# A tail that normalises tiles as they lie in DRAM, and a new order of expert units

## The chip, the cores and the metric

The kernel runs on one core of a Trainium2 chip: TensorE (matmuls), VectorE, ScalarE, GpSimd, SyncE (which here only issues DMAs) and 16 DMA engines. Time is device microseconds of one execution, the median of several. In the trace the engines are PE (its weight loads PEld), DVE, ACT, POOL and SP.

## The reference, cut to what matters

One layer of a diffusion trunk on 1024 tokens of 1024 channels, all in float32: a mixer, then a mixture of 32 experts (top 1 of 4 groups, in it the top 2 of 8 experts), then the final norm. The part that the change touches:

```
gates = einsum('tk,tke->et', weights, one_hot(eid, 32))        # two experts per token
def body(acc, (wi, wo, ge)):
    a, u = split(t @ wi, 2)                                    # wi (1024, 512)
    return acc + ((silu(a) * u) @ wo) * ge[:, None]            # wo (256, 1024)
x = x + gt_m * sum over experts                                # residual
return rmsnorm(x, final_norm_g)                                # y * rsqrt(mean(y^2) + 1e-6) * g
```

A row of the output is final only when both experts of its token have been added to the residual stream.

## The kernel before, in words

The mixer writes the residual stream x2 to a DRAM tensor `x2_d` (1024 rows of 4 KB) and the normalised rows to `h2_d`. A routing stage then makes, for each expert, a list of its tokens' row numbers (`idx`) and weights (`wtab`). The expert stage, from about 520 us to the end, works on blocks of up to 128 rows. A block holds the tokens of one expert, or of two to three experts side by side in column groups. Its steps are methods of `Block`:

- `gather` (L1623): GpSimd fetches the block's rows from `h2_d` with an indirect DMA.
- `rows` (L1644 to L1650): TensorE transposes them, VectorE and ScalarE copy the result.
- `w1` (L1659), `gate`, `gate_T`: first product, SwiGLU, transpose.
- `products2` (L1683, L1688): second product; VectorE multiplies it by the weights into a tile `y`, of which there are two.
- `scatter` (L1701): GpSimd adds the rows of `y` into `x2_d` with one accumulating indirect DMA per expert in the block. All of these write the same tensor, so each waits on GpSimd until the one before has landed.

The weights, 6 slabs of 512 KB per expert, are streamed by SyncE through a ring of 42 slabs in SBUF (L1280), in the order of use.

The unit of order is a number `u`. Units 0 to 3 are two experts of 64 rows with one scatter; 4 to 7 are two experts (up to 96 and 32 rows) and 8 to 11 two experts (up to 64 and 64), with two scatters each; 12 to 18 are one expert. Unit 18 is followed by a merged block of three parts: the overflow of the two largest experts (rows beyond 128) and one small expert, so three scatters, of which only the small expert brings new weights. `ORDER` (L45) lists the units; the last of them, 11, is treated apart. The loop over units keeps TensorE's queue in the order w1 of the next unit, transposes of the one after, w2 of this unit; the other engines' queues are sorted by a scheduler. A generator `extra_blocks` plans the overflow (which rows the merged block takes, and whether further blocks are needed); the loop takes one step of it at three places per unit, and what is left is done at once before the merged block is gathered. A loop after the tail (L1896 on) does further blocks; with these inputs it runs no turn.

The tail (from L1816) does not scatter the last block. It loads the eight tiles of `x2_d` (L1836), builds eight selection matrices from the last block's row numbers (L1841), and adds the last block's rows to each tile by matmuls: four tiles wholly in PSUM (L1857, L1861; `PSUM_X2`), four by an add on VectorE (L1863). ScalarE squares (L1875), GpSimd takes the power -1/2 (L1880), VectorE multiplies by it and by the final gain `fgb` (L1884), SyncE writes the tile out (L1885).

Of the kernel before, what the change touches and what calls it, by code (L numbers as in the profile page):

```python
# [8 lines left out]
F32 = mybir.dt.float32  # L9
F32R = mybir.dt.float32r  # L10
BF = mybir.dt.bfloat16
I32 = mybir.dt.int32
U32 = mybir.dt.uint32
AF = mybir.ActivationFunctionType
# [27 lines left out]
          *range(NS + 9, NS + 13), *range(NS + 17, E), NS + 4]  # L42

FIXED = [*range(9, 16, 2), *range(25, 32, 2)]
ORDER = [0, 1, 2, 3, 13, 4, 14, 8, 15, 5, 17, 18, 9, 6, 12, 10, 7, 16, 11]  # L45
NDB = 2
N_W0 = 3
N_W1 = 2
N_W2 = 3
NXB = 3  # L50
BIG = 1.0e6
PSUM_X2 = (0, 3, 5, 7)

O_ID, O_MF, O_MB, O_CF, O_CB, O_DM, O_LE = (128 * j for j in range(7))
O_IND = 896
# [79 lines left out]
def hybrid_layer(ctx, tc, x, c, ctx_in, c_ctx, w_ada, b_ada, norm1_g, w_in, w_decay, b_decay, gla_norm_g,  # L135
# [1095 lines left out]
    def finish_idx(ix, tokens):  # L1231
        ve.tensor_scalar(ix, tokens, BIG, None, op0=OP.add)
# [233 lines left out]
    def order_tables():  # L1466

        pe = bank(0, 2, 1)
        te.matmul(pe[0:1, 0:E], lhsT=tok0[0:E], rhs=M, start=True, stop=True)
        ve.tensor_scalar(eid, pe[0:1, 0:E], -1.0, None, op0=OP.add)  # L1470
        pt = bank(7)
        for a in range(2):
            te.transpose(pt[0:E, a * P:(a + 1) * P], tfin[:, a], ident)
        tT = mo.tile([E, 2, P], F32, name="tT", bufs=1)
        ve.tensor_copy(tT, pt[0:E, 0:2 * P].rearrange("p (a n) -> p a n", a=2))
        pt = bank(0, 2, 1)
        te.matmul(pt[:, 0:ND], lhsT=tT[:, 0], rhs=M[:, NS:], start=True, stop=True)
# [9 lines left out]
        finish_idx(here, h)  # L1487
        finish_idx(idx[:, NS:], pt[:, 0:ND])
        ve.tensor_copy(wtab[:, 0:U_Y], w[:, 0:U_Y])
        ve.tensor_copy(wtab[96:P, U_Y:], w[96:P, U_Y:])  # L1490
# [283 lines left out]
    with tc.manual_schedule(engines={mybir.EngineType.PE}):  # L1774
        for _ in range(NXB):
            gather()
        expert_order()
        next(row_order).rows()
        for n in range(-1, len(units) - 2):
            u, v, w = (units[n + k] if 0 <= n + k < len(units) else [] for k in range(3))  # L1780
            for kk in range(2):
                for b in v:
                    b.w1(kk)
            for b in u:
                b.gate_T()
            if n < 0:
                order_tables()
                gather()
                for h in range(2):
                    pt = bank(0, 2, 1)  # L1790
                    spread(pt, gm8, 4 * h)
                    sc.activation(gtm[:, h * 512:(h + 1) * 512], pt, AF.Copy)
            for b in v:
                b.w1(2)
            if n >= 1:
                next(extra, None)
            todo = len(w)
# [10 lines left out]
            if n >= 1:  # L1808
                next(extra, None)
            for b in u:  # L1810
                b.w2()
            if n >= 1:
                next(extra, None)

    u, (last,) = units[-2:]
    with tc.manual_schedule(engines={mybir.EngineType.PE, mybir.EngineType.Pool, mybir.EngineType.DVE,  # L1816
                                     mybir.EngineType.Activation}):
        for b in u:
            for j in (4, 5):
                list(b.weights(j))  # L1820
        for j in range(6):
            list(last.weights(j))
        for b in u:
            b.gate_T()
            b.w2()
        kept += staging
        fgb = next_slab()
        for h in range(2):
            pt = bank(0, 2, 1)
            spread(pt, fg8, 4 * h)  # L1830
            sc.activation(fgb[:, h * 512:(h + 1) * 512], pt, AF.Copy)
        y1 = [next_slab() for i in range(NT)]
        jk = next_slab()
# [3 lines left out]
        m = last.m  # L1837
        sel = wst.tile([P, NT, P], F32R, name="hl", bufs=2)
        yp = [wst.tile([P, D], F32R, name="wraw", tag="wraw", bufs=2)[0:m] for k in range(2)]
        for i in range(NT):  # L1840
            ve.tensor_scalar(sel[:, i], iota, float(i * P), here, op0=OP.add, op1=OP.is_equal)  # L1841
        for j in range(4):
            last.w1(j)
        last.gate()
        last.gate_T()
        y = last.products2()
        for n in range(2):
            ns = slice(n * 512, (n + 1) * 512)
            split(yp[0][:, ns], yp[1][:, ns], y[:, ns])
        pts, ss = {}, {}  # L1850

        def add(i):

            pts[i] = [bank(5, 3, 7, 6, 4, 0, 2, 1) for n in range(2)]
            on_pe = i in PSUM_X2
            for n in range(2 * on_pe):
                te.matmul(pts[i][n], lhsT=ident, rhs=y1[i][:, n * 512:(n + 1) * 512], start=True, stop=False)  # L1857
            for n in range(2):
                ns = slice(n * 512, (n + 1) * 512)
                for k in range(2):  # L1860
                    te.matmul(pts[i][n], lhsT=sel[0:m, i], rhs=yp[k][:, ns], start=(k == 0 and not on_pe), stop=(k == 1))  # L1861
                if not on_pe:
                    ve.tensor_tensor(y1[i][:, ns], pts[i][n], y1[i][:, ns], OP.add)  # L1863

        def sums(i):

            if i in PSUM_X2:
                return [(pts[i][n], slice(n * 512, (n + 1) * 512)) for n in range(2)]
            return [(y1[i], slice(0, D))]

        def tile_stats(i):
            s = mo.tile([P, 2], F32, name="ss3", bufs=3)
            ss[i] = s[:, 0:1]
            for n, (t, ns) in enumerate(sums(i)):
                sc.activation(jk[:, ns], t, AF.Square, scale=D ** -0.5, accum_out=s[:, n:n + 1])  # L1875
            if i in PSUM_X2:
                ve.scalar_tensor_tensor(ss[i], s[:, 0:1], EPS, s[:, 1:2], op0=OP.add, op1=OP.add)  # L1877
            else:
                ve.tensor_scalar(ss[i], ss[i], EPS, None, op0=OP.add)  # L1879
            gp.tensor_tensor(ss[i], ss[i], mhalf[:, 0:1], OP.pow)  # L1880

        def finish(i):
            for t, ns in sums(i):
                ve.scalar_tensor_tensor(y1[i][:, ns], t, ss[i], fgb[:, ns], op0=OP.mult, op1=OP.mult)  # L1884
            sy.dma_start(out[i * P:(i + 1) * P], y1[i])  # L1885

        for i in range(NT + 2):
            if i < NT:
                add(i)
            if 0 <= i - 1 < NT:  # L1890
                tile_stats(i - 1)
            if i >= 2:
                finish(i - 2)
# [49 lines left out]
```

## Time and profile before

| | us |
|---|---|
| three runs | 835.69, 835.94, 837.20 (median 835.94) |
| the profiled execution | 842.28 |
| its span | 840.4 |
| TensorE busy | 745.4 (89%) |
| VectorE busy | 432.0 (51%) |
| ScalarE busy | 276.7 (33%) |
| GpSimd busy | 208.7 (25%) |

The shares are means over the whole layer, in which stages with different limits follow each other. The change lies in the expert stage and in the tail, so those are read by themselves: which transfer or engine a stretch waits for, and what released the last link of it. GpSimd counts as busy only while it prepares an indirect DMA, not while the DMA runs.

### The profile page before, as it was taken

Reading aid. Unit: us, or ns where it says so; the run is one execution under the profiler, and the core shown is the slowest. Engines: PE = TensorE matmul, PEld = TensorE weight load, DVE = VectorE, ACT = ScalarE, POOL = GpSimd, SP = SyncE. Lnnn points to the kernel's source line nnn. Section 1 sums busy time; section 2 is a strip of 40 time slices with the busy share of each in tenths; the row PEclk is TensorE's granted clock in tenths of the full one; section 3 lists DMA queues with packets and bytes.
Section 4 is the critical chain, followed back from the end, with each engine's and each line's share of the span. In section 5 each row is a group of like instructions: output and inputs, shape, how many; then the busy total and the mean of one; then the engine's idle time right before and its main releaser. Section 6 shows DMA issues by size and latency. Waiting matters only on the chain. (4 is left out here: it accounts for less than half of the span.)

```text
span 840.4 us, 11818 instructions
## 1 busy us (share of the span) xinstructions
PE 745.4 (89%) x4106; PEld 502.2 (60%) x4106; DVE 432.0 (51%) x884; ACT 276.7 (33%) x526; POOL 208.7 (25%) x193
## 2 busy tenths in 40 slices
PE   4998999999999997879989575999999999989573
PEld 3676788788898966768878462434444433323232
DVE  4448856366776796654456877144123212212136
ACT  4777442345445564433433222201100101001023
POOL 2224100000001113344148544022222321222113
PEclk9899999989999998999999785999998999989788
DMA  9975875352531357554467658899999999999765
GB/s 326 290 274 181 276 236 184 120 161 90 182 133 50 135 158 282 188 180 162 136 226 257 218 213 287 305 374 347 349 393 361 338 305 336 396 344 381 241 227 201
DMA packets 78189, 206.80 MB, mean 246 GB/s; under 512 B 12460, under 2 KB 24864, under 8 KB 78129
## 3 DMA queue, kind: packets, MB, share of 16 engines
q1 hardware_dynamic: 70816, 185.45, 62.1%
q0 software_dynamic: 6560, 18.48, 9.0%
q10 hardware_dynamic: 752, 2.11, 0.7%
q8 instruction: 33, 0.54, 0.3%
q14 instruction: 28, 0.22, 0.1%
HBM read 179.81 MB, written 29.63 MB: 249 GB/s over the span
## 5 line engine op out<-in xcount | busy, mean ns | idle before, releaser
L1701 POOL DMA_INDIRECT x_d<-y,idx x26 | 38.4, 1477 | 138.0 <-DMA x_d<-y,idx 78.9
L1688 DVE SCALAR_TENSOR_TENSOR y<-bank,wtab,gtm 128x512 f32<-128x512 f32 (+1 forms) x40 | 29.7, 750 | 61.5 <-PE bank L1683 31.2
L1648 DVE COPY hh<-bank 128x512 f32<-128x512 f32 (+1 forms) x20 | 13.5, 675 | 79.2 <-PE bank L1644 79.0
L272 PE MATMUL bank<-woh,hh 128*128 128x512 f32 x124 | 52.8, 426 | 0.0
L273 PE MATMUL bank<-wol,hh 128*128 128x512 f32 x124 | 50.2, 405 | 0.8 <-DVE wol L200 0.8
L1674 ACT ACTIVATE gT<-bank 128x256 f32<-128x256 f32 (+1 forms) x20 | 7.4, 377 | 129.8 <-PE bank L1672 129.8
L274 PE MATMUL bank<-woh,hl 128*128 128x512 f32 x124 | 50.0, 403 | 0.1
L272 PE MATMUL bank<-wkh,hh 128*128 128x288 f32 (+1 forms) x144 | 42.9, 298 | 0.0
L1623 POOL DMA_INDIRECT hall<-h_d,idx x28 | 27.8, 994 | 60.1 <-PE bank L1644 52.0
L274 PE MATMUL bank<-wkh,hl 128*128 128x288 f32 (+1 forms) x144 | 42.0, 292 | 0.1
L273 PE MATMUL bank<-wkl,hh 128*128 128x288 f32 (+1 forms) x144 | 41.9, 291 | 0.0
L1659 PE MATMUL bank<-hall,hh 128*32 128x512 f32 (+4 forms) x156 | 40.9, 611 | 0.0
L200 POOL TENSOR_TENSOR wkl<-wraw,wkh 128x512 fp32r<-128x512 f32 x4 | 6.2, 1547 | 135.0 <-ACT wkh L199 135.0
L200 DVE TENSOR_TENSOR hl<-hall,hh 128x1024 fp32r<-128x1024 f32 x26 | 31.5, 1220 | 13.8 <-ACT hh L199 12.9
L1659 PE MATMUL bank<-mix,hh 128*64 128x512 f32 (+3 forms) x132 | 38.1, 600 | 0.0
L1659 PE MATMUL bank<-dS,hh 128*32 128x512 f32 (+4 forms) x88 | 37.0, 638 | 0.0
L199 ACT ACTIVATE hh<-hall 128x1024 fp32r<-128x1024 f32 x26 | 27.4, 1054 | 26.4 <-PE bank L273 22.2
L1666 DVE TENSOR_TENSOR ga<-ga,bank 128x256 f32<-128x256 f32 (+1 forms) x20 | 8.4, 421 | 48.5 <-ACT ga L1665 48.5
L272 PE MATMUL bank<-wvh,hh 128*128 128x512 f32 x80 | 32.2, 402 | 0.0
L273 PE MATMUL bank<-wvl,hh 128*128 128x512 f32 x80 | 32.0, 400 | 0.0
L274 PE MATMUL bank<-wvh,hl 128*128 128x512 f32 x80 | 31.8, 397 | 0.0
L1644 PEld LDWEIGHTS bank<-ident,hall 128*128 128x128 f32 (+1 forms) x160 | 22.7, 211 | 13.6 <-issue 11.9
(470 smaller groups left out, 1954.6 us busy)
## 6 DMA issues: line engine op xcount, KB each, us to landing
hall<-in_w_expert_in_dram SPq DMA_DIRECT2D x25, 512.0 KB
mix<-in_w_expert_in_dram SPq DMA_DIRECT2D x25, 512.0 KB
wat<-in_w_ada_dram SPq DMA_DIRECT2D x24, 512.0 KB
dS<-in_w_expert_in_dram SPq DMA_DIRECT2D x18, 512.0 KB
wraw<-in_w_ada_dram SPq DMA_DIRECT2D x16, 512.0 KB
wol<-in_w_expert_in_dram SPq DMA_DIRECT2D x14, 512.0 KB
woh<-in_w_expert_in_dram SPq DMA_DIRECT2D x13, 512.0 KB
wraw<-in_w_in_dram SPq DMA_DIRECT2D x12, 512.0 KB
```

The lines of the kernel that those rows point to most:

```text
L199: sc.activation(hi, src, AF.Copy)
L200: en.tensor_tensor(lo, src, hi.bitcast(F32), OP.subtract)
L272: te.matmul(dst, lhsT=ah[k], rhs=bh[k], start=(k == ends[0]), stop=False)
L273: te.matmul(dst, lhsT=ah[k], rhs=bl[k], start=False, stop=False)
L274: te.matmul(dst, lhsT=al[k], rhs=bh[k], start=False, stop=(k == ends[1]))
L1623: gp.indirect_dma_start(out=self.xg[q], out_offset=None, in_=h2_d, in_offset=ix, bounds_check=D - 1, oob_is_err=False)
L1644: te.transpose(pt[:, j * m:(j + 1) * m], self.xg[:, k // 2 * 256 + k % 2:(k // 2 + 1) * 256:2], ident[0:m, 0:m])
L1648: ve.tensor_copy(self.xT[:, 4:8], pt)
L1659: te.matmul(self.ph[q], lhsT=self.xT[:, k, q], rhs=w[:, j * 512:(j + 1) * 512], start=(k == 0), stop=(k == 7))
L1666: ve.tensor_tensor(ga, ga, self.ph[0:m, 256:512], OP.mult)
L1688: ve.scalar_tensor_tensor(y[:, ns], py[n][0:m], self.wt, gtm[0:m, ns], op0=OP.mult, op1=OP.mult)
L1701: gp.indirect_dma_start(out=x2_d, out_offset=ix, in_=y[q], in_offset=None, bounds_check=D - 1, oob_is_err=False, compute_op=OP.add)
```

## The change

Four things. The order of units is new: 17, 18 and the merged block come before 8, 15 and 5, and 12 before 6. The planning of the overflow takes two steps at each of its three places. The last block's row numbers are also kept as integers (`idx_l`). And the tail is rewritten: the eight tiles of `x2_d` are normalised and written out as they are, without the last block's share. The last block's rows are gathered from `x2_d` into `xl`; a matmul with the matrix `same` (1 where two rows of the block are the same token) sums its products per token; the sum is added, normalised apart, and scattered over the output after the eight tiles are written. The gain `fgb` is spread before the last but one unit's second product.

```
-ORDER = [0, 1, 2, 3, 13, 4, 14, 8, 15, 5, 17, 18, 9, 6, 12, 10, 7, 16, 11]
+ORDER = [0, 1, 2, 3, 13, 4, 14, 17, 18, 8, 15, 5, 9, 12, 6, 10, 7, 16, 11]
...
-            if n >= 1:
+            for _ in range(2 if n >= 1 else 0):
                 next(extra, None)
...
+        pt = bank(7)[0:m, 0:m]
+        te.matmul(pt, lhsT=here[0:m].to_broadcast([m, m]), rhs=ident[0:m, 0:m], start=True, stop=True)
+        ve.tensor_scalar(same, pt, here[0:m], None, op0=OP.is_equal)
...
         for i in range(NT):
             sy.dma_start(y1[i], x2_d[i * P:(i + 1) * P])
-        for i in range(NT):
-            ve.tensor_scalar(sel[:, i], iota, float(i * P), here, op0=OP.add, op1=OP.is_equal)
+        gp.indirect_dma_start(out=xl, out_offset=None, in_=x2_d, in_offset=ix, ...)
...
+        tile_stats(0)
         y = last.products2()
-            split(yp[0][:, ns], yp[1][:, ns], y[:, ns])
...
+        tile_stats(1)
+        for n in range(2):
+            te.matmul(pts[n][0:m], lhsT=same, rhs=y[:, n * 512:(n + 1) * 512], start=True, stop=True)
+        finish(0)
+        tile_stats(2)
+        finish(1)
+            ve.tensor_tensor(xl[:, ns], pts[n][0:m], xl[:, ns], OP.add)
...
+        ss_l = stats(xl, jr[0:m])
...
+        ve.scalar_tensor_tensor(xl, xl, ss_l, fgb[0:m], op0=OP.mult, op1=OP.mult)
+        for i in range(5, NT + 1):
+            if i < NT:
+                tile_stats(i)
+            finish(i - 1)
+        gp.indirect_dma_start(out=out, out_offset=ix, in_=xl, in_offset=None, ...)
```

GpSimd's queue around the merged block, before. `x_d<-y` is a scatter-add, `hall<-h_d` a gather; the first row is unit 15's scatter-add, then 5's two, 17's, 18's and the first two of the merged block (`idx_x`).

```order
L1701 DMA x_d<-y,idx 1024x1024
L1623 DMA hall<-h_d,idx 96x1024
L1623 DMA hall<-h_d,idx 32x1024
L1623 DMA hall<-h_d,idx 112x1024
L1701 DMA x_d<-y,idx 1024x1024 x2
L1623 DMA hall<-h_d,idx 64x1024
L1623 DMA hall<-h_d,idx 48x1024
L1701 DMA x_d<-y,idx 1024x1024
L1623 DMA hall<-h_d,idx 96x1024
L1623 DMA hall<-h_d,idx 32x1024
L1701 DMA x_d<-y,idx 1024x1024
L1701 DMA x_d<-y,idx_x 1024x1024 x2
```
The same place after: the first row is unit 14's scatter-add, then 17's, 18's, the merged block's three (two and one), and 8's two.

```order
L1702 DMA x_d<-y,idx 1024x1024
L1624 DMA hall<-h_d,idx 64x1024
L1624 DMA hall<-h_d,idx 48x1024
L1702 DMA x_d<-y,idx 1024x1024
L1624 DMA hall<-h_d,idx 112x1024
L1702 DMA x_d<-y,idx 1024x1024
L1702 DMA x_d<-y,idx_x 1024x1024 x2
L1624 DMA hall<-h_d,idx 96x1024
L1702 DMA x_d<-y,idx 1024x1024
L1624 DMA hall<-h_d,idx 32x1024
L1702 DMA x_d<-y,idx 1024x1024 x2
```
Units 17, 18 and the merged block stand directly behind unit 14; the scatter-adds of 8, 15 and 5, which stood ahead of them, now stand behind them.

VectorE's queue at the end, before: the last block's two products (`y`), their split into two parts, and then the tiles, here the first adds, statistics and closing multiplies.

```order
L1688 SCALAR_TENSOR_TENSOR y<-bank_6709,wtab,gtm 112x512
L1688 SCALAR_TENSOR_TENSOR y<-bank_6710,wtab,gtm 112x512
L200 TENSOR_TENSOR wraw<-y,wraw 112x512 x2
L1863 TENSOR_TENSOR mix_1159<-bank_6734,mix_1159 128x512
L1863 TENSOR_TENSOR mix_1159<-bank_6735,mix_1159 128x512
L1877 SCALAR_TENSOR_TENSOR ss_6742<-ss_6742 128x1
L1863 TENSOR_TENSOR mix_1159<-bank_6747,mix_1159 128x512
L1863 TENSOR_TENSOR mix_1159<-bank_6748,mix_1159 128x512
L1879 TENSOR_SCALAR ss_6755<-ss_6755 128x1
L1884 SCALAR_TENSOR_TENSOR mix_1159<-bank_6726,ss_6742,mix_3025 128x512
L1884 SCALAR_TENSOR_TENSOR mix_1159<-bank_6727,ss_6742,mix_3025 128x512
L1879 TENSOR_SCALAR ss_6770<-ss_6770 128x1
```
The same place after: the first tile's statistics stand ahead of the last block's products; `wol` is `xl`, the gathered rows.

```order
L1731 TENSOR_SCALAR ss_6707<-ss_6707 128x1
L1689 SCALAR_TENSOR_TENSOR y<-bank_6711,wtab,gtm 112x512
L1689 SCALAR_TENSOR_TENSOR y<-bank_6712,wtab,gtm 112x512
L1731 TENSOR_SCALAR ss_6724<-ss_6724 128x1
L1856 SCALAR_TENSOR_TENSOR mix_1159<-mix_1159,ss_6707,mix_3025 128x1024
L1731 TENSOR_SCALAR ss_6734<-ss_6734 128x1
L1856 SCALAR_TENSOR_TENSOR mix_1159<-mix_1159,ss_6724,mix_3025 128x1024
L1870 TENSOR_TENSOR wol<-bank_6728,wol 112x512
L1870 TENSOR_TENSOR wol<-bank_6729,wol 112x512
L1731 TENSOR_SCALAR ss_6742<-ss_6742 128x1
L1856 SCALAR_TENSOR_TENSOR mix_1159<-mix_1159,ss_6734,mix_3025 128x1024
L1731 TENSOR_SCALAR ss_6748<-ss_6748 112x1
```
A closing multiply is now one instruction of 1024 columns for every tile, the adds to the tiles are gone, and the last block's add and statistics stand between those of the tiles.


## Rows read from the trace of the kernel before

**Rows 1.** the chain of waits that ended last: start us, us, what

```profile
800.64 6.02 DMA x_d<-y,idx
...
806.72 3.29 DMA mix<-x_d
...
832.38 0.90 DVEq L1894
```

**Rows 2.** busy time by stretch: engines' busy us, TensorE clock, DMA share, GB/s

```profile
720.00:760.00 40.00, 37.28 (x184) 13.53 (x184) 5.72 (x10) 3.99 (x9) 11.38 (x9) 0.91 1.02 369
...
780.00:790.00 10.00, 1.36 (x9) 1.17 (x10) 1.16 (x2) 0.60 (x1) 1.91 (x2) 0.76 0.92 353
...
836.00:838.00 2.00, 0.00 (x0) 0.00 (x0) 0.00 (x0) 0.00 (x0) 0.00 (x0) 0.50 0.01 4
```

**Rows 3.** the page's costliest groups, the scatter-adds into x2_d

```profile
L1701 POOL DMA_INDIRECT x_d<-y,idx x26 | 38.4, 1477 | 138.0 <-DMA x_d<-y,idx 78.9
```

**Rows 4.** the scatter-adds on GpSimd in time: start, us, idle before and releaser

```profile
646.39 1.46 POOL L1701 DMA_INDIRECT x_d<-y,idx  x1 [6.08 <-DVE y L1688]
...
653.83 1.42 POOL L1701 DMA_INDIRECT x_d<-y,idx  x1 [5.98 <-DMA x_d<-y,idx]
...
662.26 1.59 POOL L1701 DMA_INDIRECT x_d<-y,idx  x1 [4.43 <-issue]
...
672.15 1.49 POOL L1701 DMA_INDIRECT x_d<-y,idx  x1 [4.19 <-DMA x_d<-y,idx]
...
682.96 1.34 POOL L1701 DMA_INDIRECT x_d<-y,idx  x1 [9.33 <-DMA x_d<-y,idx]
...
703.83 1.59 POOL L1701 DMA_INDIRECT x_d<-y,idx  x1 [4.07 <-DVE y L1688]
...
713.85 1.45 POOL L1701 DMA_INDIRECT x_d<-y,idx_x  x1 [8.43 <-DVE hh L1648]
...
720.57 1.35 POOL L1701 DMA_INDIRECT x_d<-y,idx_x  x1 [5.28 <-DMA x_d<-y,idx_x]
...
726.82 1.36 POOL L1701 DMA_INDIRECT x_d<-y,idx  x1 [3.52 <-DMA x_d<-y,idx_x]
...
748.82 1.47 POOL L1701 DMA_INDIRECT x_d<-y,idx  x1 [3.44 <-DMA x_d<-y,idx]
...
758.01 1.33 POOL L1701 DMA_INDIRECT x_d<-y,idx  x1 [7.73 <-DMA x_d<-y,idx]
...
782.16 1.37 POOL L1701 DMA_INDIRECT x_d<-y,idx  x1 [6.73 <-DMA x_d<-y,idx]
...
789.47 1.45 POOL L1701 DMA_INDIRECT x_d<-y,idx  x1 [5.93 <-DMA x_d<-y,idx]
...
796.51 1.33 POOL L1701 DMA_INDIRECT x_d<-y,idx  x1 [5.60 <-DMA x_d<-y,idx]
```

**Rows 5.** TensorE in time: in the planning, and after its wait near the end

```profile
633.20 0.65 PE L1583 MATMUL bank<-Vx,Sx 128*128 128x56 f32 x4 [1.09 <-DVE Sx L1582]
...
789.64 2.07 PE L220 MATMUL bank<-fg,ident 8*128 8x128 f32 x8 [8.64 <-DVE y L1688]
```

**Rows 6.** VectorE in time, the products of units 14, 8, 15 and 5

```profile
624.14 1.61 DVE L1688 SCALAR_TENSOR_TENSOR y<-bank,wtab,gtm 128x512 f32<-128x512 f32 x2 [1.31 <-PE bank L1683]
...
644.50 1.61 DVE L1688 SCALAR_TENSOR_TENSOR y<-bank,wtab,gtm 128x512 f32<-128x512 f32 x2 [1.99 <-PE bank L1683]
...
656.90 1.61 DVE L1688 SCALAR_TENSOR_TENSOR y<-bank,wtab,gtm 128x512 f32<-128x512 f32 x2 [1.88 <-PE bank L1683]
...
669.51 1.58 DVE L1688 SCALAR_TENSOR_TENSOR y<-bank,wtab,gtm 128x512 f32<-128x512 f32 x2 [2.08 <-PE bank L1683]
```

**Rows 7.** all engines in time, one instruction of each kind in the tail

```profile
818.87 1.06 ACT L1875 ACTIVATE wol<-mix 128x1024 f32<-128x1024 f32 x1
...
827.04 1.28 DVE L1884 SCALAR_TENSOR_TENSOR woh<-woh,ss,mix 128x1024 f32<-128x1024 f32 x1
...
830.39 1.46 POOL L1880 TENSOR_TENSOR ss<-ss,mhalf 128x1 f32<-128x1 f32 x1 [1.12 <-DVE ss L1877]
```

More of the change, by code (lines that the diff above doesn't have):

```diff
@@ L51 @@
 BIG = 1.0e6
-PSUM_X2 = (0, 3, 5, 7)
 O_ID, O_MF, O_MB, O_CF, O_CB, O_DM, O_LE = (128 * j for j in range(7))
@@ L1449, in hybrid_layer @@
     here = one.tile([P, 1], F32, name="here")
+    idx_l = one.tile([P, 1], I32, name="idx_l")
     eid = one.tile([1, E], I32, name="eid")
@@ L1487, in order_tables @@
         finish_idx(here, h)
+        finish_idx(idx_l, h)
         finish_idx(idx[:, NS:], pt[:, 0:ND])
@@ L1727, in stats @@
     def stats(src, junk):
-        ss = mo.tile([P, 1], F32, name="ss3", bufs=3)[0:src.shape[0]]
+        ss = mo.tile([P, 1], F32, name="ss3", bufs=4)[0:src.shape[0]]
         sc.activation(junk, src, AF.Square, accum_out=ss)
@@ L1807, in hybrid_layer @@
                 b.gate()
-            if n >= 1:
+            for _ in range(2 if n >= 1 else 0):
                 next(extra, None)
@@ L1811, in hybrid_layer @@
                 b.w2()
-            if n >= 1:
+            for _ in range(2 if n >= 1 else 0):
                 next(extra, None)
@@ L1822, in hybrid_layer @@
             list(last.weights(j))
-        for b in u:
-            b.gate_T()
-            b.w2()
         kept += staging
@@ L1831, in hybrid_layer @@
             sc.activation(fgb[:, h * 512:(h + 1) * 512], pt, AF.Copy)
+        m = last.m
+        same = mo.tile([P, P], F32, name="Sx")[0:m, 0:m]
+        pt = bank(7)[0:m, 0:m]
+        te.matmul(pt, lhsT=here[0:m].to_broadcast([m, m]), rhs=ident[0:m, 0:m], start=True, stop=True)
+        ve.tensor_scalar(same, pt, here[0:m], None, op0=OP.is_equal)
+        for b in u:
+            b.gate_T()
+            b.w2()
         y1 = [next_slab() for i in range(NT)]
-        jk = next_slab()
+        jk, jr = next_slab(), next_slab()
+        xl = next_slab()[0:m]
         sy.dma_start(tab_d, extra_tab[0])
@@ L1836, in hybrid_layer @@
             sy.dma_start(y1[i], x2_d[i * P:(i + 1) * P])
-        m = last.m
-        sel = wst.tile([P, NT, P], F32R, name="hl", bufs=2)
-        yp = [wst.tile([P, D], F32R, name="wraw", tag="wraw", bufs=2)[0:m] for k in range(2)]
-        for i in range(NT):
-            ve.tensor_scalar(sel[:, i], iota, float(i * P), here, op0=OP.add, op1=OP.is_equal)
+        ix = bass.IndirectOffsetOnAxis(ap=idx_l[0:m].bitcast(U32), axis=0)
+        gp.indirect_dma_start(out=xl, out_offset=None, in_=x2_d, in_offset=ix, bounds_check=D - 1, oob_is_err=False)
         for j in range(4):
@@ L1845, in hybrid_layer, with tile_stats, finish @@
         last.gate_T()
-        y = last.products2()
+        ss = {}
+        def tile_stats(i):
+            ss[i] = stats(y1[i], jk)
+        def finish(i):
+            ve.scalar_tensor_tensor(y1[i], y1[i], ss[i], fgb, op0=OP.mult, op1=OP.mult)
+            sy.dma_start(out[i * P:(i + 1) * P], y1[i])
+        tile_stats(0)
+        y = last.products2()
+        tile_stats(1)
+        pts = [bank(5, 3) for n in range(2)]
+        for n in range(2):
+            te.matmul(pts[n][0:m], lhsT=same, rhs=y[:, n * 512:(n + 1) * 512], start=True, stop=True)
@@ L1847, in hybrid_layer @@
+        finish(0)
+        tile_stats(2)
+        finish(1)
         for n in range(2):
             ns = slice(n * 512, (n + 1) * 512)
-            split(yp[0][:, ns], yp[1][:, ns], y[:, ns])
[L1850 to L1887, printed above, removed]
-            if i < NT:
[L1889 to L1893, printed above, removed]
+            ve.tensor_tensor(xl[:, ns], pts[n][0:m], xl[:, ns], OP.add)
+        tile_stats(3)
@@ L1894, in hybrid_layer @@
+        finish(2)
+        ss_l = stats(xl, jr[0:m])
+        finish(3)
+        tile_stats(4)
+        ve.scalar_tensor_tensor(xl, xl, ss_l, fgb[0:m], op0=OP.mult, op1=OP.mult)
+        for i in range(5, NT + 1):
+            if i < NT:
+                tile_stats(i)
+            finish(i - 1)
+        gp.indirect_dma_start(out=out, out_offset=ix, in_=xl, in_offset=None, bounds_check=D - 1, oob_is_err=False)
     nxv = nc.values_load(nxm[0:1, 0:1], min_val=NDB, max_val=NX)
```

## The prediction

> **What bounds the kernel now.** I read the chain that ended last first, then followed its first link back. The chain [rows 1] begins in a scatter-add into x2_d at 800.64 us that lands 6.02 us later, at 806.66; only then the eight loads of x2_d start, and the span ends at 840.4. So the end has two parts: what sets 806.66 (I call this moment T0), and the 33.7 us behind it.
>
> What sets T0 is not the weight stream. The DMA engines are full until 780 and 0.92 busy to 790 [rows 2], so the last weights have landed near 789, and TensorE does 1.36 us of work in those ten microseconds. Its next matmul then waited 8.64 us for VectorE [rows 5], and VectorE waited for a free y buffer, that is for an old scatter-add. The scatter-adds are the clue: GpSimd's largest idle time before them, 78.9 us, ended with the landing of the scatter-add before [rows 3]. All of them write x2_d, so each waits until the one before has landed. In time [rows 4] the reader is to see that they start one landing apart from 703.83 to the end, while at 646.39 and 703.83 it was the product (DVE y) that came last. From unit 18 on they are a queue that is never empty; its sum sets T0. The clock is no part of it: 0.91 in 720 to 760 [rows 2], where TensorE is not what the end waits for.
>
> **The change, first the order.** T0 is the start of unit 18's scatter-add plus all pieces behind it. The new order moves 17, 18 and the merged block ahead of 8, 15 and 5. That does two opposite things.
>
> Unit 18 comes earlier by the TensorE time of three units. Their products [rows 6]: 14 at 624.14, 8 at 644.50, 15 at 656.90, 5 at 669.51, so 45.4 us from 14's to 5's. But 8 took 20.4 us where 15 took 12.4: 8.0 us of that is the forced rest of the overflow planning, index matmuls that wait for VectorE one after the other (1.09 us before one of them [rows 5]), which must be done before the merged block is gathered. It stays ahead of unit 18 in the new order too, with 8 instead of 10 of its 16 index matmuls left to be forced. I take 7.0 us. Unit 18's scatter-add, at 703.83 before, then starts 45.4 - 7.0 = 38.4 us earlier, near 665.4.
>
> Behind it now stand five more pieces, 8 (two), 15 and 5 (two). From start to start [rows 4]: 653.83 - 646.39 = 7.4; 662.26 - 653.83 = 8.4; 672.15 - 662.26 = 9.9; 682.96 - 672.15 = 10.8 for 96 rows, where the other 96-row piece took 758.01 - 748.82 = 9.2, so 10.0; and 6.3 for a 32-row piece (726.82 - 720.57). Sum 42.0 us. The queue loses more than it wins: 42.0 - 38.4 = +3.6 us. One piece of the end (48 rows, 7.3 us from 782.16 to 789.47) now falls behind the end of the weight stream, where a small one took 4.1 (796.51 to 800.64): about a third of that difference, -1.0. So T0 moves by +2.6, to 809.3.
>
> Why the queue never runs dry in the new order: a two-part unit brings two pieces (about 16 us) per 12.4 us of TensorE work, and the merged block three for one expert's weights. Unit 18's piece takes 10.0 us and the merged block's 6.7, 6.3 and 6.3 (703.83 to 713.85, 720.57, 726.82 [rows 4], the third as the second), so the first piece of 8 starts at 665.4 + 29.3 = 694.7; its product comes one unit and the small merged block after 18's, by my estimate 16 to 18 us, so by 682. That lead of about 13 us is what keeps the queue full. The products behind it are then paced by the y buffers (two): block k waits for the pieces of block k-2. VectorE stands still in these waits and with it, in its queue, the copies and gates of the next unit; TensorE waits for those. That costs nothing as long as the queue ahead holds a piece, and it does. The weight ring does not suffer either: the slots that fall free later than before are asked for later still.
>
> Bounds. Five pieces of 6.3 (the smallest under load) are 31, five of 10.8 are 54; the forced planning costs 0 if the doubled pace hides it and 10 if the denser steps stall more. T0 could move by -14 to +18 with all ends at once. I take the values above, which are those of the same pieces in the row nearest to them.
>
> **The change, the tail.** Before: 33.7 us from T0 to the end, with VectorE last done at 833.28 [rows 1], 26.6 us after T0; the writes were over near 836.1 (DMA share 0.01 behind 836 [rows 2]), and the program closes 4.3 us after that.
>
> After: the first load lands at T0 + 3.3 [rows 1], its square takes 1.25 (1.06 and the read of the sum [rows 7]), so VectorE starts at T0 + 4.6. In its queue stand: the last block's two products, 1.6 (the 1.61 of [rows 6]); nine closing multiplies of 1.28 [rows 7], 11.5; the two additions, half the width each and taken together as one multiply, 1.3; nine small ones of 0.14, 1.3; and about 0.8 of gaps, because GpSimd's power takes 1.46 [rows 7], a little more than the multiply that covers it. That ends at T0 + 21.1: the removed adds and split multiplies give back 5.5 us. The square roots, TensorE's two new matmuls and the gather of 112 rows (issued at T0, wanted at T0 + 9) lie beside this. The last write lands 2.8 us later, as before, at T0 + 23.9. The DMAs come close: 8.4 MB in and out at the 369 GB/s of a full stretch [rows 2] are 22.8 us from the first load, so they end at the same moment within a microsecond.
>
> Then comes the new wait: the scatter of the last block's rows must follow all eight writes to the output, and nothing but the program's close is behind it on GpSimd. Nearest rows, without traffic: 4.1 for 32 rows [rows 4], 6.0 for 128 rows [rows 1], both with an addition. I take 5.0 for 112 rows without; under load it could be 10.8, and below 4.1 I cannot exclude. Then 4.3 for the close: T0 + 33.2, 0.5 us less than before. The index copy, the earlier `fgb` and the dropped selection matrices hang on nothing that is waited for here: TensorE and VectorE stand idle around 780 to 790 [rows 2].
>
> For such a transfer the Trainium skill (DMA: Bandwidth & Descriptors, Anatomy of one DMA) gives a fit of 2.0 us plus its bytes at 436 GB/s, 3.05 us for 112 rows of 4 KB. By that the tail would be 2.0 us shorter still. This trace does not reach it: its shortest piece, 32 rows, took 4.1 us.
>
> **Sum.** +2.6 for T0, -0.5 for the tail: +2.1 us. The profiled execution took 842.28 (span 840.4), 6.3 over the median of the runs; I expect 844.4 there, and 835.94 + 2.1 = 838.0 us as the median.
>
> **Rivals.**
> (a) The forced planning is hidden. The steps run at double pace from unit 1, so most of the VectorE chain is done when the merged block is gathered, and TensorE doesn't wait. Then unit 18 starts 7 us earlier and the queue with it: 831.0 us, faster. For it: what TensorE waits for there are small VectorE steps [rows 5], and these come earlier. Against: the gather also comes three blocks earlier, and 8 index matmuls are still left in one go.
> (b) The tail's last scatter is cheap: the program's close of 4.3 us, which begins at the last write, runs beside its 5.0 us of landing instead of behind it, about 4 us less: 834.0. Against it: the close must drain the queue that carries the scatter.
> (c) The y buffers starve the queue: VectorE waits so long that a unit's product comes after its turn, TensorE falls back in clock as it did in 720 to 760 (0.91 [rows 2]), and one unit's two-piece time is lost in part, 8 us: 846 us, slower.
> (d) T0 doesn't come from the queue but from the weight stream, so the order changes nothing and only the tail counts: 835.4. Against it: the stream is over at 789, T0 is 806.66.
>
> **Chances.** Forecast (queue and tail as summed, 834 to 842): 0.45. (a) 0.25, (b) 0.12, (c) 0.13, (d) 0.05. A change of under 0.2% (1.7 us) is what a measurement can't tell from none. The forecast's own spread of 4 us puts 0.07 of its 0.45 in faster, 0.13 in same, 0.25 in slower; (a) gives 0.23 to faster and 0.02 to same; (b) 0.07 faster, 0.04 same, 0.01 slower; (c) all slower; (d) same, 0.04, and 0.01 faster. Sum 0.38, 0.23, 0.39. The range leaves out a tenth on each side: 828 to 846.
>
> **What will show it.** Right: scatter-adds one landing apart without a break from unit 18's (near 665) to T0; T0 near 809; VectorE's last multiply 21 us after T0, one GpSimd scatter to the output some 3 us after it, the end 33 us after T0. Wrong: a GpSimd scatter-add that waits for DVE y after 680 (the queue ran dry: then T0 is set by units 10, 7 and 16, and comes before 800); unit 18's piece before 660; a gap of TensorE in the planning much over 8 us or none.

## The result and the profile after

The changed kernel takes 844.97 us (median of 13 runs), the one before 836.13 us in 13 runs of the same comparison: ratio 1.0092, interval 1.0066 to 1.0118, slower by 5.5 to 9.9 us. Forecast was 838.0, with 828 to 846 as the range. The ratios here and below leave out slow executions (the variants had a single one, 2391.83 us in e12).

The profiled execution of after has a span of 842.3 us, before 840.4. That is only 1.9 us (-3.58 ahead of the first scatter-add, +3.74 from there to the loads, +1.74 behind), since what comes ahead of the experts, which the change doesn't touch, varies: in the fourteen profiles of this study the first scatter-add starts between 543.3 and 552.2. So I count from the first scatter-add (the expectations below count from the first product, about 2.5 us earlier), and split at the issue of the first load of x2_d, which comes 0.06 us behind T0. Before, GpSimd's first scatter-add and SP's loads:

```profile
552.24 1.63 POOL L1701 DMA_INDIRECT x_d<-y,idx  x1 [4.59 <-DMA dS<-in_w_expert_in_dram]
```

```profile
806.72 1.75 SPq L1836 DMA_DIRECT2D mix<-x_d  x4
```

After, the scatter-adds on GpSimd in time (start, us, idle before and releaser), with the two new transfers at the end, and SP's loads; they answer to [rows 4]:

```profile
548.66 1.63 POOL L1702 DMA_INDIRECT x_d<-y,idx  x1 [4.59 <-issue]
...
649.14 1.60 POOL L1702 DMA_INDIRECT x_d<-y,idx  x1 [4.05 <-DVE y L1689]
...
661.83 1.56 POOL L1702 DMA_INDIRECT x_d<-y,idx  x1 [5.15 <-DVE y L1689]
671.55 1.44 POOL L1702 DMA_INDIRECT x_d<-y,idx_x  x1 [8.15 <-issue]
...
693.07 1.43 POOL L1702 DMA_INDIRECT x_d<-y,idx  x1 [4.92 <-DMA x_d<-y,idx]
701.42 1.43 POOL L1702 DMA_INDIRECT x_d<-y,idx  x1 [6.91 <-DMA x_d<-y,idx]
...
709.34 1.59 POOL L1702 DMA_INDIRECT x_d<-y,idx  x1 [3.92 <-DMA x_d<-y,idx]
...
719.63 1.47 POOL L1702 DMA_INDIRECT x_d<-y,idx  x1 [6.16 <-issue]
728.88 1.34 POOL L1702 DMA_INDIRECT x_d<-y,idx  x1 [7.78 <-DMA x_d<-y,idx]
...
735.59 1.45 POOL L1702 DMA_INDIRECT x_d<-y,idx  x1 [4.00 <-issue]
...
783.43 1.37 POOL L1702 DMA_INDIRECT x_d<-y,idx  x1 [6.50 <-DMA x_d<-y,idx]
...
796.46 1.31 POOL L1702 DMA_INDIRECT x_d<-y,idx  x1 [4.98 <-DMA x_d<-y,idx]
800.54 1.56 POOL L1702 DMA_INDIRECT x_d<-y,idx  x1 [2.77 <-issue]
807.61 1.04 POOL L1845 DMA_INDIRECT wol<-x_d,idx_l  x1 [5.51 <-issue]
...
834.04 1.03 POOL L1881 DMA_INDIRECT out_dram<-wol,idx_l  x1 [6.31 <-DMA out_dram<-woh]
```

```profile
806.88 1.75 SPq L1843 DMA_DIRECT2D mix<-x_d  x4
```

The reader is to see three things. From 548.66 to the loads it is 258.2 us, before 254.5: +3.7. From the loads to the end it is 842.3 - 806.88 = 35.4 us, before 33.7: +1.7. And no scatter-add behind unit 18's (661.83) has VectorE's product as its releaser, as 649.14 and 661.83 still have: the queue is never empty, as forecast. Two rows of the page answer to this ([rows 3] for the first): the idle time behind scatter-adds is 75.0 us (78.9 before), and VectorE now waits 60.2 us for y buffers (21.0 before).

```profile
L1689 DVE SCALAR_TENSOR_TENSOR y<-bank,wtab,gtm 128x512 f32<-128x512 f32 (+1 forms) x40 | 29.3, 749 | 90.6 <-DMA x_d<-y,idx 60.2
L1702 POOL DMA_INDIRECT x_d<-y,idx x26 | 38.5, 1483 | 136.2 <-DMA x_d<-y,idx 75.0
```

The chain of waits that ended last, in answer to [rows 1], is now the last write of a tile, and then the scatter to the output:

```profile
829.75 3.34 DMA out_dram<-woh
...
834.04 1.03 POOL out_dram L1881
```

VectorE in the tail of after:

```profile
811.27 0.15 DVE L1731 TENSOR_SCALAR ss<-ss 128x1 f32<-128x1 f32 x1 [17.21 <-ACT wol L1730]
...
812.88 1.28 DVE L1856 SCALAR_TENSOR_TENSOR mix<-mix,ss,mix 128x1024 f32<-128x1024 f32 x1
817.02 0.15 DVE L1731 TENSOR_SCALAR ss<-ss 128x1 f32<-128x1 f32 x1 [2.85 <-ACT wol L1730]
...
824.26 1.28 DVE L1856 SCALAR_TENSOR_TENSOR woh<-woh,ss,mix 128x1024 f32<-128x1024 f32 x1 [0.38 <-POOL ss L1732]
...
827.24 2.48 DVE L1856 SCALAR_TENSOR_TENSOR woh<-woh,ss,mix 128x1024 f32<-128x1024 f32 x2 [0.38 <-POOL ss L1732]
```

The 2.85 us in its third row end with ScalarE's square of the third tile, which itself waited for that tile's load:

```profile
815.84 1.06 ACT L1730 ACTIVATE wol<-mix 128x1024 f32<-128x1024 f32 x1 [3.10 <-DMA mix<-x_d]
```

VectorE's chain starts 4.4 us behind the loads' issue, stands still for these 2.85 us, and ends at 829.72, 22.8 us behind the issue. The last write lands 3.4 us later (833.09), the scatter starts at 834.04, and the program is over 8.3 us after that.

### The profile page after: what moved, and what is told of

The parts are those of the page before. It is cut to its first block, busy times and chain, and to the rows that moved or that the text cites. A ratio compares the mean times of both kernels' runs of the same rounds, so it can differ in the third digit from the quotient of the medians.

```text
span 842.3 us, 11715 instructions
## 1 busy us (share of the span) xinstructions
PE 729.2 (87%) x4064; PEld 488.4 (58%) x4064; DVE 426.5 (51%) x868; ACT 275.4 (33%) x518; POOL 212.0 (25%) x196
## 5 line engine op out<-in xcount | busy, mean ns | idle before, releaser
L1689 DVE SCALAR_TENSOR_TENSOR y<-bank,wtab,gtm 128x512 f32<-128x512 f32 (+1 forms) x40 | 29.3, 749 | 90.6 <-DMA x_d<-y,idx 60.2
L199 DVE TENSOR_TENSOR hl<-hall,hh 128x1024 fp32r<-128x1024 f32 x26 | 31.6, 1221 | 14.7 <-ACT hh L198 14.6
L1660 PE MATMUL bank<-dS,hh 128*64 128x512 f32 (+4 forms) x92 | 38.3, 628 | 0.0
L271 PE MATMUL bank<-wvh,hh 128*128 128x512 f32 x80 | 32.2, 402 | 0.0
L1660 PE MATMUL bank<-mix,hh 128*32 128x512 f32 (+3 forms) x136 | 32.0, 598 | 0.0
L1660 PE MATMUL bank<-hall,hh 128*32 128x512 f32 (+3 forms) x124 | 31.5, 598 | 0.0
L408 PE MATMUL bank<-wph,phh 128*128 128x512 f32 x64 | 26.2, 409 | 2.4 <-ACT phh L198 2.0
```

Of the source, the lines that this page charges most:

```text
L271: te.matmul(dst, lhsT=ah[k], rhs=bh[k], start=(k == ends[0]), stop=False)
L408: te.matmul(acc[j], lhsT=hh[:, ts], rhs=wph[k], start=(k == 0), stop=False)
L1660: te.matmul(self.ph[q], lhsT=self.xT[:, k, q], rhs=w[:, j * 512:(j + 1) * 512], start=(k == 0), stop=(k == 7))
L1689: ve.scalar_tensor_tensor(y[:, ns], py[n][0:m], self.wt, gtm[0:m, ns], op0=OP.mult, op1=OP.mult)
```

## The experiments

Profiles of all kernels, in us; "to loads" is from the first scatter-add's start to the loads' issue, "to end" from there to the span's end. Ratios are to the kernel before, from runs beside it on the same chip.

| kernel | order, planning steps per unit, tail | to loads | to end | ratio (interval) |
|---|---|---|---|---|
| before | old, 3, old | 254.5 | 33.7 | |
| e2 | old, 3, new | 253.1 | 35.8 | 1.0030 (1.0002 to 1.0059) |
| e3 | old, 6, old | 250.7 | 32.1 | 0.9973 (0.9948 to 0.9998) |
| e9 | old, 4, old | 251.0 | 33.5 | 0.9959 (0.9933 to 0.9985) |
| e12 | old, 4, old with two tiles on TensorE | 250.5 | 32.2 | 0.9955 (0.9925 to 0.9986) |
| e5 | two-part units early, 6, old | 250.5 | 33.4 | 0.9989 (0.9959 to 1.0018) |
| e1 | new, 6, old | 258.0 | 33.4 | 1.0026 (0.9994 to 1.0057) |
| after | new, 6, new | 258.2 | 35.4 | 1.0092 (1.0066 to 1.0118) |
| e8 | after once more | 257.2 | 35.2 | 1.0079 (1.0049 to 1.0110) |
| e7 | after, three y buffers | 258.4 | 35.5 | 1.0080 (1.0045 to 1.0116) |
| e4 | after, no last scatter | 258.0 | 29.5 | 0.9998 (0.9970 to 1.0026) |
| e10 | after, no gather in the tail | 258.9 | 33.4 | 1.0073 (1.0046 to 1.0100) |
| e6 | after, half the loads in the tail | 261.0 | 34.0 | 1.0115 (1.0066 to 1.0165) |
| e11 | after, one scatter-add less | 251.5 | 35.0 | 1.0017 (0.9983 to 1.0051) |

**The parts of the change (e1, e2, e3).** e1 is before with the new ORDER and the doubled pace (the second hunk stands at all three places):

```diff
-ORDER = [0, 1, 2, 3, 13, 4, 14, 8, 15, 5, 17, 18, 9, 6, 12, 10, 7, 16, 11]
+ORDER = [0, 1, 2, 3, 13, 4, 14, 17, 18, 8, 15, 5, 9, 12, 6, 10, 7, 16, 11]
...
-            if n >= 1:
+            for _ in range(2 if n >= 1 else 0):
                 next(extra, None)
```

> The kernel before with the new order of units and the doubled pace of the overflow planning; the tail of before stays. Theory Q (the scatter-adds are one queue; unit 18's start moved by -38.4 us and the pieces behind it grew by 42.1 us in the two profiles): T0 comes about 3.7 us later after the first product than before (261 us instead of 257), the tail keeps its 33.7 us, the time rises by 3 to 4 us, ratio about 1.004. Rival T (the order costs nothing, the whole 8.8 us sits in the tail): ratio 1.000. Rival O (the order costs all of it, the profiled run of before was an unusually long one): ratio 1.009 or more.

Measured: 837.18 us, 258.0 us to the loads, tail 33.4. Theory Q's two stretches are met. O is outside the ratio's interval; T is inside it, but the stretch to the loads speaks against it. e2 is after with both of these undone:

> The changed kernel with the old order of units and the old pace; only the tail is new. Theory Q: T0 stays at 257 us after the first product, the tail takes 35.5 us as in the changed kernel's profile instead of 33.7: +1.8 us, ratio 1.002. Inside it: DMA share 0.97 from the first landing to the last write, VectorE's last multiply some 3 us before the last write. Rival T: ratio 1.009. Rival of the forecast (the tail is 0.5 us shorter): 0.9994.

Measured: 839.44 us, 253.1 and 35.8: the tail's +2 is there in full with the old order, as with the new one (35.4 in after against 33.4 in e1); T's 1.009 and the forecast's 0.9994 are outside the interval. e3 has the second hunk of e1 alone:

> The kernel before with nothing changed but the pace of the overflow planning, doubled; old order, old tail. With the old order the planning then has three more blocks of time, so it should be finished before the merged block is gathered and TensorE's wait of 8 us at 630 goes. Theory Q: between unit 14's and unit 8's scatter-add the queue stood empty, so everything behind comes earlier by nearly those 8 us, less 0 to 2 for waits that fill up: T0 249 to 251 us after the first product, 828 to 830 us, ratio 0.991 to 0.993. Rival W (the end hangs on the weight stream or on the y buffers, not on when the queue gets its pieces): under 2 us, ratio 0.998 to 1.000.

Measured: 833.59 us, 3.7 us less to the loads than before, 2.4 less than e2, which has before's order and pace. In e3 GpSimd's first scatter-add and unit 18's, and then VectorE's products of units 3, 13 and 4 (start, us, idle before and releaser):

```profile
544.66 1.63 POOL L1701 DMA_INDIRECT x_d<-y,idx  x1 [4.59 <-issue]
...
690.70 1.59 POOL L1701 DMA_INDIRECT x_d<-y,idx  x1 [4.08 <-DVE y L1688]
```

```profile
579.28 1.61 DVE L1688 SCALAR_TENSOR_TENSOR y<-bank,wtab,gtm 128x512 f32<-128x512 f32 x2 [2.15 <-PE bank L1683]
...
593.90 1.61 DVE L1688 SCALAR_TENSOR_TENSOR y<-bank,wtab,gtm 112x512 f32<-112x512 f32 x2 [2.01 <-PE bank L1683]
...
607.28 1.61 DVE L1688 SCALAR_TENSOR_TENSOR y<-bank,wtab,gtm 128x512 f32<-128x512 f32 x2 [1.96 <-PE bank L1683]
```

The 8 us wait is gone: unit 8's product follows unit 14's by 11.7 us instead of 20.4. But six steps in a unit cost TensorE something themselves: units 13 and 4 follow after 14.6 and 13.4 instead of 12.4 and 11.7. So unit 18's scatter-add comes 5.5 us earlier (146.0 us after the first instead of 151.6), not 8, and the pieces behind it give 1.8 of that back. Theory Q had the kind and twice the size; W, with under 2 us, is out by the profiles, though not by much; the interval of the ratio reaches to 0.9998 and doesn't exclude it. Since e1 and e3 differ by the order alone, the new order costs 258.0 - 250.7 = 7.3 us at the doubled pace, which gave the old order 3 to 4. What that pace gives the new order isn't shown: no run has the new order with the old pace.

**Four planning steps (e9).** e3's second hunk at one of three places only.

> The kernel before with four planning steps per unit instead of three (the doubled pace has six); order and tail of before. Four steps in seven units are 28, just enough for all of them before the merged block is gathered. In the doubled pace's profile the 8 us wait before unit 8's product was gone, but two earlier products each came 1 to 2.4 us later than their usual 12.2 us. Theory P (the steps cost TensorE something when many stand in one unit): with four the early products keep their 12.2 to 12.7 us and the wait of 8 us shrinks to 0 to 2, T0 5 to 7 us earlier than before counted from the first product (250 to 252 us instead of 257), ratio 0.992 to 0.994. Rival R (the gain is limited by what the queue loses further on, not by the steps): the same 253 us as with the doubled pace, ratio 0.997.

Measured: 833.04 us; the early products nearly kept their pace (12.4 and 12.9 for units 13 and 4), the wait shrank to about 1 (unit 8's product follows unit 14's by 13.3), and T0 was still 251.0 us behind the first scatter-add, 253.5 behind the first product. That is R's number, though the ratio's interval holds part of P's as well. R's reason is only half of it: unit 18's scatter-add comes 146.1 us behind the first, as in e3, so of the 8 us some 2.5 are lost again on TensorE ahead of it with four steps as with six, and 2 go behind it, where the queue takes 104.9 us instead of 102.9.

**A queue fed early (e5).**

```diff
-ORDER = [0, 1, 2, 3, 13, 4, 14, 8, 15, 5, 17, 18, 9, 6, 12, 10, 7, 16, 11]
+ORDER = [0, 1, 2, 3, 4, 8, 13, 5, 9, 14, 6, 17, 18, 15, 12, 10, 7, 16, 11]
```

> The kernel before with the doubled pace and another order of units: 0, 1, 2, 3, 4, 8, 13, 5, 9, 14, 6, 17, 18 with the merged block, 15, 12, 10, 7, 16, 11; old tail. The two-part units, whose pieces take longer to land than TensorE needs for the unit, stand early and the single ones between and behind them, so that the queue never runs dry after unit 3. Theory Q: T0 is unit 4's start (near 601) plus the sum of all pieces behind it as the two profiles have them, 189 us: 790 to 795 instead of 806.7, so 12 to 16 us earlier, 820 to 824 us, ratio 0.981 to 0.986. Rival W (the weight stream, over near 789, with the y buffers' waits on TensorE before it, sets the end): T0 at 800 or later, ratio 0.992 or more. If the order doesn't matter at all: 1.000.

Measured: 834.27 us; 4 us less to the loads than before, not 12 to 16, and only 0.2 less than e3. The scatter-adds from unit 4 to the loads took 198.3 us (598.50 to 796.84), not 189. Those of units 17 and 18:

```profile
698.79 1.59 POOL L1701 DMA_INDIRECT x_d<-y,idx  x1 [4.03 <-DVE y L1688]
...
710.48 1.59 POOL L1701 DMA_INDIRECT x_d<-y,idx  x1 [4.90 <-DVE y L1688]
```

Both waited for a product: unit 17's came 24.1 us behind unit 6's (672.76 to 696.90), where the same step takes 19.6 in after. TensorE in that stretch had to wait for weights:

```profile
684.24 2.54 PE L1659 MATMUL bank<-wq,hh 128*128 128x512 f32 x6 [1.48 <-DMA wq<-in_w_expert_in_dram]
...
689.31 1.99 PE L1659 MATMUL bank<-St,hh 128*128 128x512 f32 x4 [0.93 <-DMA St<-in_w_expert_in_dram]
```

So the queue did start earlier, but TensorE had caught up with the stream of weights, and its products then came late for the queue. The two waits in these rows are 2.4 of the 4.5 us by which unit 17's product was late; and the two late products cost the queue some 4 of the 9 us, the rest being pieces that took longer than those the sum was made of, as unit 7's first with 8.6 us instead of 7.0. My theory Q failed here in size; what rival W says of the weights is a part of it, though T0 lay at 796.8 and not behind 800.

**Is T0 the queue? (e11, e7).** In e11 unit 15's product isn't scattered:

```diff
-            self.scatter(self.products2())
+            y = self.products2()
+            if self is not units[ORDER.index(15)][0]:
+                self.scatter(y)
```

> The changed kernel without unit 15's scatter-add, 128 rows (left out: these rows of the sum lack unit 15's share); its weights, matmuls and product stay. That piece took 10.3 us in the queue of the changed kernel's profile (709.34 to 719.63). Theory Q (from unit 18's piece on T0 is the sum of the queue): T0 comes 9 to 10 us earlier, 250 to 252 us from the first product to the loads' issue instead of 260.7, the time falls by as much against the changed kernel, ratio to before about 0.996 to 0.998. Rival W (weights or TensorE set T0): under 3 us, ratio 1.005 or more.

Measured: 837.95 us; 251.5 us to the loads, 6.5 less than the 258.0 of the new order's other profiles (after, e1, e4, e7, e8), where Q had 9 to 10 and W under 3. The ratio, 1.0017, lies between the two. At these rows the queue now ran dry:

```profile
711.49 1.47 POOL L1704 DMA_INDIRECT x_d<-y,idx  x1 [2.75 <-DVE y L1689]
...
743.42 1.51 POOL L1704 DMA_INDIRECT x_d<-y,idx  x1 [4.09 <-DVE y L1689]
```

So the queue sets T0, but T0 isn't its plain sum: of the 10.3 us that were taken out 6.5 arrived at its end. The two waits for products took about 1.8 of the rest (the pieces ahead of these two rows last 9.2 and 8.0 us, in after 7.9 and 7.6), and about 2 went to pieces further on that took longer, as unit 10's two with 8.8 and 7.3 us instead of 7.9 and 6.6. In e7 `y` has three buffers (`bufs=3`, and `N_W2 = 2`):

> The changed kernel with three y buffers instead of two, and one slab less in the ring of weights for it (room). VectorE waits 60 us in all for a y buffer there. Theory Q: these waits cost nothing, since the queue ahead always holds a piece; products come earlier, pieces do not: T0 260 to 262 us after the first product, ratio as the changed kernel, 1.007 to 1.009. Rival Y (the waits for y starve the queue or slow the stream of weights): T0 4 us or more earlier, ratio 1.004 or less.

Measured: 842.72 us, 258.4 to the loads. On the page VectorE's row has 44.7 us of idle time, 42.7 of it for TensorE, so 2.0 at most are left of the 60.2 us of waits for y; T0 stayed:

```profile
L1689 DVE SCALAR_TENSOR_TENSOR y<-bank,wtab,gtm 128x512 f32<-128x512 f32 (+1 forms) x40 | 29.9, 750 | 44.7 <-PE bank L1684 42.7
```

These waits cost nothing in this order, as the forecast said; rival (c) is refuted.

**The tail (e4, e6, e10, e12).** e4 drops the last instruction:

```diff
-        gp.indirect_dma_start(out=out, out_offset=ix, in_=xl, in_offset=None, bounds_check=D - 1, oob_is_err=False)
```

> The changed kernel without its last instruction, the scatter of the last block's summed rows to the output (left out: these rows of the output lack the last block's share). Theory S (the scatter waits for all eight writes and its landing stands alone on the path): the end comes by its issue, 0.95, and its landing earlier, 4.9 us in all, so the span ends 30.5 us after the loads are issued instead of 35.4, and the time lies 4.9 us under the changed kernel's (near 840, ratio to before 1.003). Rival C (the program's close, 4.3 us, runs beside the landing): 1 us or less.

Measured: 837.3 us, the span's end 29.5 us behind the loads' issue, 5.9 less than after; the times differ by 6.8 to 7.7. So the scatter stands wholly on the path, rival (b) is refuted, and without it the new tail is 3.7 us shorter than the old (33.2 on average). In e6 four loads leave the tail:

```diff
-        for i in range(NT):
+        for i in range(4, NT):
+            sy.dma_start(y1[i], h2_d[i * P:(i + 1) * P])
+        for i in range(4):
             sy.dma_start(y1[i], x2_d[i * P:(i + 1) * P])
```

> The changed kernel, in which the last four tiles are loaded from the normalised input of the expert stage, long before the scatter-adds end (left out: these four tiles of the output are then not the right sums). Instructions on VectorE, ScalarE, GpSimd and TensorE stay the same; 2.1 MB of loads leave the tail, 5.7 us at the 366 GB/s that it moves. Theory D (the new tail is bound by the DMA engines: share 0.97 from 810 to 830, the last write 26.2 us after the loads' issue though VectorE's multiplies need 18): the last write comes 4 to 5.7 us earlier, span end 30 to 31 us after the loads' issue instead of 35.4. Rival V (VectorE's chain sets the last write, as the forecast had it with 21.1 + 2.8): at most the 1 to 2 us of the wait for the third tile's load.

Measured: the end 34.0 us behind the issue, 1.4 less than after. The busy times of one stretch of the tail (columns as in [rows 2]: PE, PEld, DVE, ACT, POOL, clock, DMA share, GB/s), first after, then e6:

```profile
820.00:830.00 10.00, 0.00 (x0) 0.00 (x0) 8.68 (x12) 5.31 (x10) 5.70 (x6) 0.50 0.97 393
```

```profile
820.00:830.00 10.00, 0.00 (x0) 0.00 (x0) 8.96 (x15) 5.64 (x10) 5.98 (x6) 0.56 0.64 257
```

VectorE's busy time in them is nearly the same (8.68 and 8.96 us). From the third tile's statistics to the last multiply it took 12.7 us in both. So a DMA share of 0.97 wasn't the bound: a third of the traffic went and the last multiply came 0.7 us nearer to the issue. Theory D falls, V holds. (The time itself, 845.88 us in four runs, didn't fall, since 2.8 us more passed up to the loads: the moved loads lay beside the last scatter-adds, of which unit 7's first took 8.2 us instead of 6.4.) In e10 the gather leaves the tail:

```diff
-        gp.indirect_dma_start(out=xl, out_offset=None, in_=x2_d, in_offset=ix, bounds_check=D - 1, oob_is_err=False)
+        sy.dma_start(xl, h2_d[0:m])
```

> The changed kernel, in which the last block's 112 rows are not gathered behind T0 but loaded in a row from another tensor long before (left out: these rows of the output are then not the right sums). Half the loads taken away moved the end by 1.4 us only and VectorE still waited 2.0 us for the third tile. Theory G (the gather, 0.46 MB on its own queue, stands in the way of the third tile's load, which lands 9 us after the first issue while the second lands within 4.7): the third tile lands 2 to 4 us earlier, VectorE's wait of 2.85 us there goes and its last multiply ends 20 to 21 us after the loads' issue instead of 22.8; the time falls by 2 to 3 us against the changed kernel. Rival L (the loads of all tiles share the engines and land late by themselves): at most 1 us.

Measured: 841.8 us; the end 33.4 us behind the issue, 2.0 less than after, the last multiply 21.5 us behind it instead of 22.8.

```profile
817.72 0.15 DVE L1731 TENSOR_SCALAR ss<-ss 128x1 f32<-128x1 f32 x1 [1.60 <-ACT wol L1730]
```

Its wait for the third tile is 1.60 us, against 2.85 in after and 3.27 in e8: about half of it is the gather's, half the loads' own, as far as one profile shows it. G and L share it; by time the gain isn't shown (ratio 1.0073, the changed kernel's 1.0079 in e8). e12 is e9 with another tail constant:

```diff
-PSUM_X2 = (0, 3, 5, 7)
+PSUM_X2 = (3, 6)
```

> Order and tail of before, four planning steps per unit, and in the old tail two tiles (3 and 6) instead of four (0, 3, 5, 7) whose loaded rows TensorE adds itself with an identity matrix. In the profile of before VectorE's first addition of the tail starts 9.5 us after the loads' issue, because TensorE first passes tile 0 through four such matmuls of 0.94 us at the low clock; behind that both are busy to the end. Theory H (the start of VectorE's chain is what counts): without tile 0's four matmuls it starts 4 us earlier, and has two tiles more to add, 2 x 1.15 us: the last multiply 1 to 3 us nearer to the loads' issue than 26.6 us, the span end 31 to 32.5 us behind it instead of 33.7, ratio 0.992 to 0.995 beside 0.996 for the four steps alone. Rival K (the third tile's load, or VectorE's longer chain, takes it back): no gain, 0.996 or more.

Measured: 833.19 us, as e9's 833.04. VectorE's first wait of this tail and the longest behind it:

```profile
804.04 2.66 DVE L1863 TENSOR_TENSOR mix<-bank,mix 128x512 f32<-128x512 f32 x4 [4.63 <-DMA mix<-x_d]
...
814.56 1.29 DVE L1863 TENSOR_TENSOR woh<-bank,woh 128x512 f32<-128x512 f32 x2 [2.57 <-PE bank L1861]
```

VectorE starts 3.3 us behind the loads' issue instead of 9.1 in e9 (803.35 - 794.26), then waits for a load (0.96 us) and for TensorE (2.57 us here), and its last multiply ends 25.8 us behind the issue instead of 26.2. The end, 32.2 us behind the issue, lies in H's range, but e3 reached 32.1 with the old tail: a gain isn't shown, and K stands. e9 and e12 are the fastest kernels of the study, 0.4% under before.

**Once more (e8).**

> The changed kernel once more, unchanged, beside the others on the same chip. The profiles of its parts add to +3.5 us (order and pace, up to T0) and +2 us (tail), 5.5 us, while its first comparison gave 8.8 us with an interval from 5.5 to 9.9. If the parts are all there is: ratio 1.006 to 1.007, and 260 to 261 us from the first product to the loads' issue, 35.4 us from there to the end. If order and tail together cost something that neither costs alone: 1.009 or more again, with one of these two stretches longer.

Measured: 844.14 us, 257.2 and 35.2. By the profiles' stretches the parts explain the whole: new order and pace 258.0 (after, e1, e4, e7, e8) against 253.8 (before, e2), +4.2; new tail 35.5 (after, e2, e7, e8) against 33.2 (before, e1, e3, e5, e9), +2.3; 6.5 us in all, within both intervals (5.5 to 9.9 and 4.1 to 9.2). By time the parts come to less, since the ratios of e1 and e2 add to 0.56%, 4.7 us, but each is known only to 2.5 us. Whether there is a microsecond or two beyond it stays open.

## Why the prediction was right about the queue, and wrong about the tail

**T0, unit 18's start: right.** Forecast -38.4; from the first scatter-add to unit 18's it is 151.6 us before and 113.2 after: -38.4. The two estimates in it held too. The planning still stalls TensorE, now ahead of unit 13, whose product comes 20.1 us behind unit 3's where unit 3's came 12.2 behind unit 2's, so 7.9 us (forecast 7.0), and rival (a) was wrong: the doubled pace hides it only in the old order (e3). VectorE's products of units 3, 13, 14 and 17 in after, in answer to [rows 6]:

```profile
583.28 1.61 DVE L1689 SCALAR_TENSOR_TENSOR y<-bank,wtab,gtm 128x512 f32<-128x512 f32 x2 [2.15 <-PE bank L1684]
...
603.41 1.61 DVE L1689 SCALAR_TENSOR_TENSOR y<-bank,wtab,gtm 112x512 f32<-112x512 f32 x2 [1.88 <-PE bank L1684]
...
627.62 1.61 DVE L1689 SCALAR_TENSOR_TENSOR y<-bank,wtab,gtm 128x512 f32<-128x512 f32 x2 [1.89 <-PE bank L1684]
...
647.25 1.61 DVE L1689 SCALAR_TENSOR_TENSOR y<-bank,wtab,gtm 128x512 f32<-128x512 f32 x2 [1.88 <-PE bank L1684]
```

Unit 17's step of 19.6 us holds the merged block's first matmuls, as it did before.

**T0, the pieces behind it: right within 1.2 us.** The five pieces of 8, 15 and 5 took 42.5 us (693.07 to 735.59; forecast 42.0). Units 9 to 16 took 71.3 us instead of 73.1, where the forecast had a relief of 1.0 at the stream's end; but e2, with the old order, has 71.7, so the relief isn't clear of the spread between profiles. Unit 18 and the merged block took 31.2 instead of 29.8 (29.7 in e2), which I hadn't considered; my 29.3 for them put the third piece of the merged block at 6.3, and it took 6.8 in before. Together +42.2 where I had +41.0. T0 so moved by +3.7 in the pair of profiles and by +4.2 over seven, forecast +2.6.

**The tail: the step that failed.** The forecast had VectorE's queue end at T0 + 21.1, and so the tail 0.5 us shorter. It ended at + 22.9. The sum put the wait for the loads behind the first at nothing, and the third tile's 2.85 us was there; the start and the instructions themselves came 1.1 us under the sum. In before this wait was covered: TensorE's matmuls kept VectorE from starting until 816.23, when by my estimate 3.3 of the 4.2 MB had moved (9.5 us at the 346 GB/s of that stretch), and that cover went with the matmuls. The last write landed 3.4 us behind the multiply, where I had 2.8, read from the DMA share. Scatter and close, 9.3 us in the forecast, took 9.2 (833.09 to 842.3). That makes 35.4 where I had 33.2. My second estimate, that the DMA engines end at the same moment, fell short with the first, and e6 shows that they weren't the bound.

**The sum.** +2.1 forecast, +6.5 by the stretches, +8.8 (5.5 to 9.9) by the time. Of the 4.4 us between the first two the tail has 2.8 (+2.3 where I had -0.5) and T0 1.6 (+4.2 where I had +2.6). Slower had a chance of 0.39 against 0.38 for faster, so the forecast hardly committed itself to the direction that came out. The measured 844.97 lies in the range but beyond the forecast's own 834 to 842; of the named cases it is nearest to (c), 846, whose mechanism e7 refutes, so that the range held it is partly luck. Rivals (a) and (b), 0.37 together, were wrong, (a) by the row of unit 13 and (b) by e4. Rival (d) falls with e11: one piece less moved T0 by 6.5 us.

## What to carry to other kernels

Where transfers must follow one another, the end is the start of the unbroken queue plus its sum: ask of a new order which work it puts ahead of that start, which behind it, and whether what feeds the queue keeps up. The sum is an estimate, since what a piece takes depends on what stands beside it (in e11 a piece of 10.3 us gave 6.5). A faster first step of a tail meets what the slow one had hidden, here a load; count the waits that were covered, not only the instructions that go. And compare stretches between two marks of the program rather than spans: the part that nobody touched moved by more than the change.

## What the hardware showed unexpectedly

A DMA share near 1 didn't mean a bound: with 0.97 and 393 GB/s, and with 0.64 and 257 GB/s, the same VectorE chain ran in the same time. The scatter of 112 rows to the output without an addition cost 5.9 us of the span with nothing else running; 0.95 of it passed before it started (833.09 to 834.04), which leaves some 5 us, where a scatter-add of 128 rows took 6.0 [rows 1]. A scatter-add under the weight stream did not have one price: the 96-row pieces of units 5 and 6 took 10.8 and 9.2 us before, and 9.2 (719.63) and 8.3 (760.51) after.
